# Matrix inversions on four partition groups, and the last one moved beside the output projection

## The chip, the cores and the metric

The kernel runs on one core of a Trainium2 chip. The core has five engines that work side by side, each with its own queue of instructions that it takes in order: TensorE (PE, matrix products), VectorE (DVE), ScalarE (ACT), GpSimd (POOL) and SyncE (SP, which here only issues transfers). Transfers between device memory (DRAM) and the core's memory (SBUF) are issued by ACT, POOL or SP into their own queues and carried by 16 DMA engines. The metric is the time of one execution on the device, in microseconds (us), as the median of several runs.

## The reference

The computation is a trunk of two layers over a sequence of 512 positions, with a model width of 1024. Cut to what matters:

```python
for l in range(DEPTH):                       # two layers
    h = rms_norm(x, norm_mix[l])
    if l % 2 == 0:                           # layer 0
        u = h @ w_in_even[e]
        ya = hgrn2_mix(aq, af, ai, ag, ...)  # columns of u
        yb = rwkv7_mix(ub, ...)              # the other columns
        y = jnp.concatenate([ya, yb], axis=-1) @ w_out_even[e]
    else:                                    # layer 1: S5 and mLSTM
        y = jnp.concatenate([yc, yd], axis=-1) @ w_out_odd[o_]
    x = x + y
    x = x + swiglu(rms_norm(x, norm_ffn[l]), ...)
return rms_norm(x, norm_final)
```

RWKV-7 is a recurrence over positions, in eight heads of 64:

```python
def step(state, inp):
    r_t, w_t, k_t, v_t, a_t, b_t = inp
    sa = jnp.einsum("bhvk,bhk->bhv", state, a_t)
    state = (state * w_t[:, :, None, :] + sa[..., None] * b_t[:, :, None, :]
             + v_t[..., None] * k_t[:, :, None, :])
    return state, jnp.einsum("bhvk,bhk->bhv", state, r_t)
```

## The kernel before

Weights stream from DRAM on SP's queue in pieces of 128 x up to 1024 (`raw`). Every matrix is split into a high and a low half (`hi` is a cast on ACT, L375; `lo` a subtraction, on DVE or POOL, L376), and each matrix product of two such operands is three products of 128 x 128 by 128 x 512 (`mm3`), all at line 292. `d`, `m` and `r` are the PSUM tiles: `d` of the large projections, `m` of HGRN2, `r` of RWKV-7; there are two `d` buffers.

Layer 0 runs three kinds of work side by side. The first is the input projection with HGRN2 (`dense`, F): lora parts L, RWKV-7's projections P0 to P3, HGRN2's blocks H0 to H3. HGRN2 forms decays `e` (POOL makes e from c, DVE multiplies them by u and k) which PE reads (m<-e), and a block's result `y` is stored to DRAM (scr_ya, L837). The second is RWKV-7 in chunks of 64 positions, for two halves g of the sequence and two groups q of four heads: `rwp` prepares (gates, keys, the triangular 64 x 64 blocks `pb`), `inv` is `rw_inverse`, and `rwd` is `rw_solve` for two pairs of heads, then `rw_chain` for both pairs beside each other. The third is the output projection.

`rw_prep` stores the diagonal 32 x 32 triangular blocks of `pb` to DRAM (scr_a, issued by ACT). `rw_inverse(q, g)` loads 32 of them on POOL's queue as `iu`, one block per partition, with 1024 elements each, and inverts each unit triangular block: at step j of 30, row j's multipliers times row j go to all rows above j. That is a product `ti` (L987) and an addition (L989) of j x (31 - j) elements on 32 partitions. It stores the inverse to scr_u (L991). `rw_solve` loads it as `ub` (L1000, eight transfers of 32 x 4 x 32, on POOL's queue), and PE multiplies (r<-y,ub), corrects by `amb` and multiplies again to give `wu`. `rw_chain` runs four chunks: PE sums a chunk (r<-kr,vbd, r<-pb,wu, r<-ar,hs), ACT and DVE copy half of it each to `sb`, PE transposes it (r<-con,sb, L1049), DVE scales it into the state `hs`. Then it normalises over a head (r<-kr,con, y, kr), multiplies by the gate (r<-la,lora) and leaves the result in `bon` (L1077).

Programs of these kinds of work are generators that yield a virtual cost. `weave` advances the stream with the least cost so far; `beside` alternates between streams, `then` runs one after the other, `scaled` multiplies the costs. The table `PRM` sets it all: `prog` lists the stages of layer 0, each woven to its end, with the place up to which F runs in it; `m` are the factors of inv, rwp and rwd; `e` is the factor of the RWKV-7 work beside the output projection; `dq` says which queue issues the transfers of the RWKV-7 part (ACT for scr_a's stores, POOL for the rest). The scheduler of the language then orders the instructions of each engine at build time.

In the kernel before, the last stage of `prog` is inv(1, 1) beside rwd(1, 0), with no F beside it. After the stages the eight x tiles are loaded (`xtiles`, L520, on ACT's queue, into the memory that HGRN2 has left). `outa` then reloads six of the eight 128-column groups of y from DRAM (`yraw`, L1164, on SP's queue, through two buffers), splits them into `ysp` (yhl[k]; the groups come in the order 0, 1, 2, 4, 5, 3, and 3 is H3's result), and runs, for each of the eight output tiles n, fifteen products of groups 0, 1, 2, 4, 5 (d<-ysp) and the addition to x[n] (L1173), which frees the `d` buffer. It is woven with the last rwd(1, 1). At the end the results of rwd(1, *) for groups 6 and 7 are split from `bon` into yhl[6] and yhl[7], and a second pass over n (weights wO0b) does the nine products of groups 3, 6 and 7.

The functions that the diff touches:

Of the kernel before, what the change touches and what calls it, by code (L numbers as in the profile page):

```python
# [198 lines left out]
PRM = {'c': (0, 1, 2, 3), 'seq': ['L', 'P0', 'P1', 'H0', 'P2', 'P3', 'H1', 'H2', 'H3'], 'm': {'inv': 1.728, 'rwp': 1.6, 'rwd': 0.675}, 'prog': [[('F', 'P1')], [('rwp', 0, 0), ('F', 'H0')], [('inv', 0, 0), ('rwp', 0, 1), ('F', 'P2')], [('inv', 0, 1), ('rwd', 0, 0), ('F', 'H1')], [('rwd', 0, 1), ('rwp', 1, 0), ('F', 'H2')], [('inv', 1, 0), ('rwp', 1, 1), ('F', 'H3')], [('inv', 1, 1), ('rwd', 1, 0)]], 'e': 0.2, 'k': 8.0, 'dq': 'aggg', 'j': 0.9, 'eng': {('h8', 2): 'G', ('c5', 0, 0): 'S', 'h7': 'G', 'c7': 'S', ('p2', 3, 0): 'S', ('c1', 0, 0): 'S', ('c1', 1, 0): 'S', 'c6': 'V', 'c4': 'S', ('c1', 2, 0): 'V', 'h3': 'V', ('p14', 3, 0): 'V', ('h8', 1): 'G', ('c7', 1): 'V', ('c5', 1): 'V', 'h5': 'V', ('c8', 2): 'G', ('p2', 0): 'S', ('s4', 1, 0): 'S', 's2': 'S', 'c2': 'S', 'z1': 'G', 'z4': 'G', 'z6': 'G', ('z5', 0): 'V', ('a6', 3): 'G', 'p10': 'V', 'z9': 'V', 'p13': 'S', ('z2', 1): 'G', ('z0', 4): 'S', ('z1', 3): 'V', 'h13': 'V', ('a6', 2): 'G', ('z0', 1): 'G', ('h12', 1): 'V', ('n2', 2): 'V', ('p11', 1): 'S', ('a2', 2): 'V'}, 'pu': (2, 4, 5, 6, 7, 9, 12, 13, 36), 'i': 1.0, 'h': 0.7, 'f': 1.4, 'pr': {}}  # L199
# [3 lines left out]
def trunk(ctx: ExitStack, tc: tile.TileContext, A, out, dbg=None, start=0):  # L203
# [451 lines left out]
    def layer0():  # L655
# [323 lines left out]
        def rw_inverse(q, g):  # L979

            iu = pl.tile([32, 32, 32], F32, tag="iu", name="iu")
            dq(1).dma_start(iu, scr_a[q, g].rearrange("p h b c s t -> (p h b c) s t"))
            G.memset(iu.rearrange("p a b -> p (a b)")[:, 0:1024:33], 1.0)
            for j in range(1, 31):
                n = 31 - j
                t3 = pl.tile([32, N2], F32, tag="ti", name="ti")[:, 0:j * n].rearrange("p (a b) -> p a b", b=n)
# [2 lines left out]
                G.tensor_tensor(iu[:, 0:j, j + 1:], iu[:, 0:j, j + 1:], t3, ADD)  # L989
# [759 lines left out]
```

## Time and profile before

| | |
|---|---|
| runs | 1464.06 us median of 3 (1461.65 to 1466.17) |
| profiled execution | 1462.31 us, of which the span of the trace is 1460.5 us |
| granted TensorE clock, mean | 0.976 of full speed |
| busy share of the span | PE 96%, PE weight loads 78%, DVE 66%, ACT 47%, POOL 24% |
| DMA | 133.39 MB, 91 GB/s on average |
| inversions on POOL, first to last operation, us from the start | 90.93 to 133.39, 156.37 to 193.60, 272.78 to 314.10, 333.60 to 375.02 |
| layer 0's last RWKV-7 product (r<-la,lora) | 409.86 us |

A row of the timeline gives the start, the duration, the engine, the line and what it writes from what it reads. "[0.62 <-DVE wu L281]" says that the engine had been idle for 0.62 us ahead of the row and that DVE's instruction at line 281 that writes wu released it. A group's row gives the busy time and the mean of one in ns, then the idle time ahead. TensorE's granted clock (PEclk) is the share of full speed that the chip allowed it in a stretch. Instructions that issue a transfer are not counted as busy.

### The profile page before, as it was taken

The numbers are of one execution on the slowest core, as the hardware profiler recorded it, in microseconds if no ns is written. First come the engines' busy times: TensorE is split into PE (matmuls) and PEld (weight loads), VectorE is DVE, ScalarE is ACT, GpSimd is POOL, SyncE is SP. The second block draws the span as 40 slices with busy tenths as digits, with TensorE's granted clock in tenths as the row PEclk, the third lists the DMA queues.
The fourth block names the chain that finished last, engine by engine and source line by source line (L and its number), as shares of the span: only waits on it lengthen the run. The fifth ranks groups of instructions, "written<-read, shape, count | busy, mean of one in ns | idle before, by whom it ended". The sixth has DMA issues, their size and how long they took to land.

```text
span 1460.5 us, 19910 instructions
## 1 busy us (share of the span) xinstructions
PE 1400.2 (96%) x6668; PEld 1136.9 (78%) x6668; DVE 961.2 (66%) x2041; ACT 681.1 (47%) x1594; POOL 354.0 (24%) x538
## 2 busy tenths in 40 slices
PE   8989999988999999999999899999999999999996
PEld 5877878766787788888888678766678888888885
DVE  7588679899688656555444688678776555554433
ACT  7554565636365333344333333477554434433332
POOL 5367650668420333110010542100020000000001
PEclk9988999999999999999999999999999999999998
DMA  5311221111323332333343842410133233333331
GB/s 180 94 38 46 64 72 52 30 46 58 118 84 97 101 116 91 113 108 106 105 125 105 206 113 80 116 58 28 56 105 90 99 101 96 92 102 94 93 114 61
DMA packets 51142, 133.39 MB, mean 91 GB/s; under 512 B 10640, under 2 KB 16272, under 8 KB 50784
## 3 DMA queue, kind: packets, MB, share of 16 engines
q1 hardware_dynamic: 38656, 116.86, 26.4%
q0 software_dynamic: 3024, 7.26, 2.1%
q10 hardware_dynamic: 9360, 8.00, 1.8%
q8 instruction: 53, 0.87, 0.2%
q14 instruction: 49, 0.40, 0.1%
HBM read 121.71 MB, written 10.39 MB: 90 GB/s over the span
## 4 chain that ended last, share of the span: by engine, by line
PE 76%; DVE 11%; POOL 4%; ACT 4%; DMA 2%; issue 2%; ACTq 0%; SPq 0%; DVEq 0%; POOLq 0%
PE d L292 63%; PE m L292 7%; PE r L292 5%; DVE lo L376 2%; POOL iu L989 1%; POOL ti L987 1%; DVE e L277 1%; DMA raw<-in_wV_dram 1%; ACT s L253 1%; DVE hl L467 1%; DVE ks L277 1%; ACT hi L375 0%; DVE u L277 0%; POOL ks L277 0%; DMA x<-in_xT_dram 0%
## 5 line engine op out<-in xcount | busy, mean ns | idle before, releaser
L375 ACT CAST hi<-raw 128x256 fp32r<-128x256 f32 (+1 forms) x809 | 317.4, 402 | 502.1 <-PE d L292 446.8
L376 DVE TENSOR_TENSOR lo<-raw,hi 128x256 fp32r<-128x256 f32 (+1 forms) x774 | 348.3, 460 | 280.5 <-ACT hi L375 269.6
L292 PE MATMUL d<-hh,hi 128*128 128x512 f32 x1088 | 436.1, 401 | 3.6 <-DVE ur L1086 2.4
L292 PE MATMUL d<-hh,lo 128*128 128x512 f32 x1088 | 431.4, 397 | 0.0
L292 PE MATMUL d<-hl,hi 128*128 128x512 f32 x1088 | 430.2, 395 | 0.0
L292 PEld LDWEIGHTS d<-hh,hi 128*128 128x128 f32 x1088 | 207.1, 190 | 48.0 <-DVE ur L1086 3.0
L292 PEld LDWEIGHTS d<-hh,lo 128*128 128x128 f32 x1088 | 206.8, 190 | 43.7 <-issue 1.5
L292 PEld LDWEIGHTS d<-hl,hi 128*128 128x128 f32 x1088 | 206.9, 190 | 43.3 <-issue 2.3
L292 PE MATMUL d<-ah,hi 128*128 128x512 f32 x330 | 128.4, 389 | 0.0
L292 PE MATMUL d<-al,hi 128*128 128x512 f32 x330 | 128.4, 389 | 0.0
L292 PE MATMUL d<-ah,lo 128*128 128x512 f32 x330 | 128.4, 389 | 0.0
L1718 POOL TENSOR_TENSOR x<-x,f 128x256 f32<-128x256 f32 x6 | 5.2, 889 | 358.8 <-issue 352.3
L292 PE MATMUL d<-ysp,hi 128*128 128x512 f32 x224 | 75.3, 411 | 2.7 <-DVE x L1685 1.5
L473 POOL TENSOR_TENSOR rstd<-rstd,sq 128x512 f32<-128x512 f32 x21 | 28.8, 1373 | 196.8 <-ACT sq L253 196.7
L989 POOL TENSOR_TENSOR iu<-iu,ti 32x30 f32<-32x30 f32 (+14 forms) x120 | 70.8, 590 | 9.2
L292 PEld LDWEIGHTS d<-ah,hi 128*128 128x128 f32 x330 | 61.9, 188 | 13.0
L292 PEld LDWEIGHTS d<-ah,lo 128*128 128x128 f32 x330 | 61.9, 188 | 12.8
L292 PEld LDWEIGHTS d<-al,hi 128*128 128x128 f32 x330 | 61.9, 188 | 12.8
L987 POOL TENSOR_TENSOR ti<-iu 32x30 f32<-32x30 f32 (+14 forms) x120 | 68.9, 574 | 9.0
L292 PEld LDWEIGHTS d<-ysp,hi 128*128 128x128 f32 x224 | 42.2, 193 | 12.9 <-DVE x L1685 2.3
L292 PE MATMUL d<-ysp,lo 128*128 128x512 f32 x112 | 45.5, 406 | 0.0
L1197 DVE TENSOR_TENSOR g<-d,g 128x512 f32<-128x512 f32 x42 | 29.0, 691 | 24.1 <-PE d L292 24.1
(490 smaller groups left out, 2043.0 us busy)
## 6 DMA issues: line engine op xcount, KB each, us to landing
raw<-in_wGU_dram SPq DMA_DIRECT2D x88, 512.0 KB, 3.6
raw<-in_wD_dram SPq DMA_DIRECT2D x32, 512.0 KB, 3.5
raw<-in_wA_dram SPq DMA_DIRECT2D x16, 512.0 KB, 3.7
raw<-in_wB_dram SPq DMA_DIRECT2D x13, 512.0 KB, 3.7
raw<-in_wD_dram SPq DMA_DIRECT2D x16, 384.0 KB, 3.1
raw<-in_wV_dram SPq DMA_DIRECT2D x6, 512.0 KB, 5.7
raw<-in_wQ_dram SPq DMA_DIRECT2D x6, 512.0 KB, 3.6
raw<-in_wK_dram SPq DMA_DIRECT2D x6, 512.0 KB, 3.7
```

The costliest lines, as they stand in the source:

```text
L253: a = S.activation(o, i, f, bias=bias, scale=scale)
L277: on(op, i, j).tensor_tensor(o, a, b, f)
L292: T.matmul(o, w, a, start=start, stop=stop)
L375: S.copy(h, src)
L376: eng.tensor_tensor(l, src, h.bitcast(F32), SUB)
L467: V.scalar_tensor_tensor(self.hl[:, k, :], x, pc(self.g, k), self.hh[:, k, :].bitcast(F32), MUL, SUB)
L473: self.eng.tensor_tensor(self.rstd, self.rstd, sq, ADD)
L987: G.tensor_tensor(t3, iu[:, j:j + 1, j + 1:].to_broadcast([32, j, n]), iu[:, 0:j, j:j + 1].to_broadcast([32, j, n]), MUL)
L989: G.tensor_tensor(iu[:, 0:j, j + 1:], iu[:, 0:j, j + 1:], t3, ADD)
L1197: V.tensor_tensor(g1, pu_, g1, MUL)
L1718: G.tensor_tensor(x[k][:, t], x[k][:, t], r_, MUL)
```

## The change

There are two edits. First, `rw_inverse` copies its 32 blocks four times, into four groups of 32 partitions (`iu`, 128 x 1024), and gives group k of the 32 rows those with r = k mod 4 to work on (`iw`, 128 x 8 x 32). A step's two operations then run on 128 partitions with m = (j+3)//4 rows each. The loads are eight instead of one, in pairs of one `iw` (eight rows of 32 elements per block, so pieces of 128 bytes) and one `iu`; at the end the four groups get their ones on the diagonal and are stored with four transfers. The step's cost in the weave is 0.6 instead of 1.2. Second, the last stage is taken out of `prog`, and its work stands at the head of the stream beside the output projection, whose factor e goes from 0.2 to 0.4.

```diff
 PRM = 
 ...
-[('inv', 1, 0), ('rwp', 1, 1), ('F', 'H3')], [('inv', 1, 1), ('rwd', 1, 0)]], 'e': 0.2,
+[('inv', 1, 0), ('rwp', 1, 1), ('F', 'H3')]], 'e': 0.4,
 ...
         def rw_inverse(q, g):
-            iu = pl.tile([32, 32, 32], F32, tag="iu", name="iu")
-            dq(1).dma_start(iu, scr_a[q, g].rearrange("p h b c s t -> (p h b c) s t"))
-            G.memset(iu.rearrange("p a b -> p (a b)")[:, 0:1024:33], 1.0)
+            iu = pl.tile([P, 32, 32], F32, tag="iu", name="iu")
+            iw = pl.tile([P, 8, 32], F32, tag="iw", name="iw")
+            blocks = scr_a[q, g].rearrange("p h b c s t -> (p h b c) s t")
+            for k in range(4):
+                w = slice(32 * k, 32 * k + 32)
+                dq(1).dma_start(iw[w], blocks.rearrange("n (r k) t -> n k r t", k=4)[:, k])
+                dq(1).dma_start(iu[w], blocks)
             for j in range(1, 31):
-                n = 31 - j
-                t3 = pl.tile([32, N2], F32, tag="ti", name="ti")[:, 0:j * n].rearrange("p (a b) -> p a b", b=n)
-                G.tensor_tensor(t3, iu[:, j:j + 1, j + 1:].to_broadcast([32, j, n]),
-                                iu[:, 0:j, j:j + 1].to_broadcast([32, j, n]), MUL)
-                G.tensor_tensor(iu[:, 0:j, j + 1:], iu[:, 0:j, j + 1:], t3, ADD)
-                yield 1.2
-            dq(2).dma_start(scr_u[q, g].rearrange("p h b c s t -> (p h b c) s t"), iu)
+                n, m = 31 - j, (j + 3) // 4
+                t3 = pl.tile([P, 80], F32, tag="ti", name="ti")[:, 0:m * n].rearrange("p (a b) -> p a b", b=n)
+                G.tensor_tensor(t3, iu[:, j:j + 1, j + 1:].to_broadcast([P, m, n]),
+                                iw[:, 0:m, j:j + 1].to_broadcast([P, m, n]), MUL)
+                G.tensor_tensor(iw[:, 0:m, j + 1:], iw[:, 0:m, j + 1:], t3, ADD)
+                yield 0.6
+            for k in range(4):
+                w = slice(32 * k, 32 * k + 32)
+                G.memset(iw[w].rearrange("p a b -> p (a b)")[:, k:256:36], 1.0)
+                dq(2).dma_start(scr_u[q, g].rearrange("p h b c s t -> (p h b c) s t")
+                                .rearrange("n (r k) t -> n k r t", k=4)[:, k], iw[w])
 ...
-        weave((scaled(rwd(1, 1), PRM.get("e", 1.0)), None), (outa(), "end"))
+        weave((scaled(build(("then", ("beside", ("inv", 1, 1), ("rwd", 1, 0)), ("rwd", 1, 1))), PRM.get("e", 1.0)), None), (outa(), "end"))
```

Lines below the inversion stand ten lines later in the changed kernel (L1049 becomes L1059, L1164 becomes L1174). PE, DVE, ACT and SP have the same instructions in both kernels; POOL has 52 more. On PE the order differs in two places only: beside the first inversion with H0, and from the last solution but one to the end of the RWKV-7 work.

The first place is POOL's queue at the last inversion, inv(1, 1) beside H3. In the kernel before, one load (`iu`) is followed by three of HGRN2's five operations on `e`, then by the inversion:

```order
L982 DMA iu<-scr_a 32x1024
L277 TENSOR_TENSOR e<-c 128x8x32
L277 TENSOR_TENSOR e<-c 128x16x16
L277 TENSOR_TENSOR e<-c 128x32x8
L983 MEMSET iu 32x32
L987 TENSOR_TENSOR ti<-iu 32x30
L989 TENSOR_TENSOR iu<-iu,ti 32x30
```

In the changed kernel, on POOL at the same place, eight loads stand among all five operations on `e`, ahead of the inversion:

```order
L987 DMA iw<-scr_a 32x8x32
L988 DMA iu<-scr_a 32x1024
L277 TENSOR_TENSOR e<-c 128x8x32
L277 TENSOR_TENSOR e<-c 128x16x16
L987 DMA iw<-scr_a 32x8x32
L277 TENSOR_TENSOR e<-c 128x32x8
L988 DMA iu<-scr_a 32x1024
L987 DMA iw<-scr_a 32x8x32
L277 TENSOR_TENSOR e<-c 128x64x4
L277 TENSOR_TENSOR e<-c 128x128x2
L988 DMA iu<-scr_a 32x1024
L987 DMA iw<-scr_a 32x8x32
```

Before, the other two operations on `e` stood after fourteen of the inversion's operations; now the first operation of the inversion stands behind all five and one more load of iu.

The second place is ACT's queue at the head of rwd(1, 0)'s chain, where `wu` is the end of the solution, `x` the loads of the x tiles and `sb` the copies that the chain waits for. The kernel before:

```order
L281 COPY wu_245<-r 64x8x64
L375 CAST hi<-raw 128x256
L375 CAST hi<-raw 128x128
L281 COPY sb_249<-r 64x64 x2
L281 COPY sb_247<-r 64x64
L375 CAST hi<-raw 128x256
L520 DMA x_3981<-in_xT_dram 128x512
L520 DMA x_3982<-in_xT_dram 128x512
L281 COPY sb_247<-r 64x64
L281 COPY sb_249<-r 64x64 x2
L520 DMA x_3983<-in_xT_dram 128x512
```

The changed kernel, on ACT from the same copy to wu (five of the eight loads are shown, they stand in a row):

```order
L520 DMA x_3768<-in_xT_dram 128x512
L520 DMA x_3769<-in_xT_dram 128x512
L520 DMA x_3770<-in_xT_dram 128x512
L520 DMA x_3771<-in_xT_dram 128x512
L520 DMA x_3772<-in_xT_dram 128x512
L375 CAST ysp<-yraw 128x512
L281 COPY sb_247<-r 64x64
L281 COPY sb_249<-r 64x64 x2
```

The eight loads, which stood between copies to sb, and the cast of the last reloaded group of y, which stood behind all of them, now stand ahead of the first copy to sb.

The third place is PE's queue where that chain makes its first transpose (r<-con,sb). In the kernel before, a few products of the output projection stand among the chain's:

```order
L292 MATMUL r_3809<-pb2_272,wu1_245 128x128
L292 MATMUL d_4162<-ysp_4025,hi_4049 128x512
L292 MATMUL d_4162<-ysp_4026,hi_4049 128x512
L292 MATMUL r_3809<-kr2_273,vbd2_275 128x128
L1049 MATMUL r_3814<-con_72,sb0_247 128x128
L292 MATMUL r_3801<-kr0_255,vbd0_257 128x128
```

In the changed kernel seventeen of them stand in a row there; the last of these rows on PE, with `d_4063` the third output tile and `d_4183` the fourth:

```order
L292 MATMUL d_4063<-ysp_3821,hi_3949 128x512
L292 MATMUL d_4063<-ysp_3822,hi_3949 128x512
L292 MATMUL d_4063<-ysp_3821,lo_3950 128x512
L292 MATMUL d_4183<-ysp_3797,hi_4051 128x512
L292 MATMUL d_4183<-ysp_3798,hi_4051 128x512
L1059 MATMUL r_3995<-con_72,sb0_247 128x128
L292 MATMUL r_3979<-kr0_255,vbd0_257 128x128
```

Counted over the whole region, 47 products of the output projection stood ahead of rwd(1, 1)'s first product with ub (r<-y1,ub0) and now 60 do. Behind the last r<-la,lora, 39 stood ahead of the first that reads yhl[6], and now 26 do.

More of the change, by code (lines that the diff above doesn't have):

```diff
@@ L196, in _layout @@
     return o
-PRM = {'c': (0, 1, 2, 3), 'seq': ['L', 'P0', 'P1', 'H0', 'P2', 'P3', 'H1', 'H2', 'H3'], 'm': {'inv': 1.728, 'rwp': 1.6, 'rwd': 0.675}, 'prog': [[('F', 'P1')], [('rwp', 0, 0), ('F', 'H0')], [('inv', 0, 0), ('rwp', 0, 1), ('F', 'P2')], [('inv', 0, 1), ('rwd', 0, 0), ('F', 'H1')], [('rwd', 0, 1), ('rwp', 1, 0), ('F', 'H2')], [('inv', 1, 0), ('rwp', 1, 1), ('F', 'H3')], [('inv', 1, 1), ('rwd', 1, 0)]], 'e': 0.2, 'k': 8.0, 'dq': 'aggg', 'j': 0.9, 'eng': {('h8', 2): 'G', ('c5', 0, 0): 'S', 'h7': 'G', 'c7': 'S', ('p2', 3, 0): 'S', ('c1', 0, 0): 'S', ('c1', 1, 0): 'S', 'c6': 'V', 'c4': 'S', ('c1', 2, 0): 'V', 'h3': 'V', ('p14', 3, 0): 'V', ('h8', 1): 'G', ('c7', 1): 'V', ('c5', 1): 'V', 'h5': 'V', ('c8', 2): 'G', ('p2', 0): 'S', ('s4', 1, 0): 'S', 's2': 'S', 'c2': 'S', 'z1': 'G', 'z4': 'G', 'z6': 'G', ('z5', 0): 'V', ('a6', 3): 'G', 'p10': 'V', 'z9': 'V', 'p13': 'S', ('z2', 1): 'G', ('z0', 4): 'S', ('z1', 3): 'V', 'h13': 'V', ('a6', 2): 'G', ('z0', 1): 'G', ('h12', 1): 'V', ('n2', 2): 'V', ('p11', 1): 'S', ('a2', 2): 'V'}, 'pu': (2, 4, 5, 6, 7, 9, 12, 13, 36), 'i': 1.0, 'h': 0.7, 'f': 1.4, 'pr': {}}
+PRM = {'c': (0, 1, 2, 3), 'seq': ['L', 'P0', 'P1', 'H0', 'P2', 'P3', 'H1', 'H2', 'H3'], 'm': {'inv': 1.728, 'rwp': 1.6, 'rwd': 0.675}, 'prog': [[('F', 'P1')], [('rwp', 0, 0), ('F', 'H0')], [('inv', 0, 0), ('rwp', 0, 1), ('F', 'P2')], [('inv', 0, 1), ('rwd', 0, 0), ('F', 'H1')], [('rwd', 0, 1), ('rwp', 1, 0), ('F', 'H2')], [('inv', 1, 0), ('rwp', 1, 1), ('F', 'H3')]], 'e': 0.4, 'k': 8.0, 'dq': 'aggg', 'j': 0.9, 'eng': {('h8', 2): 'G', ('c5', 0, 0): 'S', 'h7': 'G', 'c7': 'S', ('p2', 3, 0): 'S', ('c1', 0, 0): 'S', ('c1', 1, 0): 'S', 'c6': 'V', 'c4': 'S', ('c1', 2, 0): 'V', 'h3': 'V', ('p14', 3, 0): 'V', ('h8', 1): 'G', ('c7', 1): 'V', ('c5', 1): 'V', 'h5': 'V', ('c8', 2): 'G', ('p2', 0): 'S', ('s4', 1, 0): 'S', 's2': 'S', 'c2': 'S', 'z1': 'G', 'z4': 'G', 'z6': 'G', ('z5', 0): 'V', ('a6', 3): 'G', 'p10': 'V', 'z9': 'V', 'p13': 'S', ('z2', 1): 'G', ('z0', 4): 'S', ('z1', 3): 'V', 'h13': 'V', ('a6', 2): 'G', ('z0', 1): 'G', ('h12', 1): 'V', ('n2', 2): 'V', ('p11', 1): 'S', ('a2', 2): 'V'}, 'pu': (2, 4, 5, 6, 7, 9, 12, 13, 36), 'i': 1.0, 'h': 0.7, 'f': 1.4, 'pr': {}}
 @with_exitstack
```

## The prediction

> **What bounds the kernel now.** I read first the page's busy rows, then a table of stretches through layer 0, then what TensorE waited for there, and last the rows of the engines that the change touches.
>
> ```profile
> span 1460.5 us, 19910 instructions
> PE 1400.2 (96%) x6668; PEld 1136.9 (78%) x6668; DVE 961.2 (66%) x2041; ACT 681.1 (47%) x1594; POOL 354.0 (24%) x538
> ```
>
> TensorE (PE) is busy 96% of the span and the change removes no matmul, so it can win only PE's idle time and the time that PE runs at a lower clock, near the inversions. The next table shows how much there is; its columns are the length of the stretch, busy time of PE, weight loads, DVE, ACT and POOL, then PE's granted clock.
>
> ```profile
> core 0: us, PE busy (x) PEld busy (x) DVE busy (x) ACT busy (x) POOL busy (x), PEclk, DMA share, GB/s
> 88.00:142.00 54.00, 49.05 (x248) 40.06 (x247) 46.11 (x88) 31.45 (x79) 44.49 (x77) 0.84 0.14 40
> 142.00:214.00 72.00, 70.48 (x407) 58.19 (x405) 52.41 (x117) 40.16 (x104) 45.07 (x81) 1.00 0.25 72
> 258.00:342.00 84.00, 72.98 (x422) 59.91 (x419) 76.82 (x168) 47.93 (x121) 59.12 (x102) 0.88 0.14 39
> 342.00:384.00 42.00, 36.62 (x237) 30.14 (x237) 34.64 (x70) 18.85 (x50) 33.83 (x55) 1.00 0.34 111
> 384.00:410.00 26.00, 25.62 (x166) 21.64 (x166) 14.28 (x34) 10.43 (x32) 3.28 (x6) 1.00 0.18 54
> ```
>
> I call the first of these A, the second B, the third D, and the last two together E. Idle PE time is 4.95 us in A, 1.52 in B, 11.02 in D, 5.38 up to 384 us and 0.38 after it. Besides, the clock of 0.84 and 0.88 costs at most 0.16 x 49.05 = 7.8 us in A and 0.12 x 72.98 = 8.8 us in D. VectorE (DVE) is the fullest engine after PE: 76.82 of 84 us in D. And the waits of PE from 88 to 416 us name it:
>
> ```profile
> engine line waited for: us in total, times, longest us
> PE m L292 <- DVE e L277: 5.4, 7, 2.4
> PE r L959 <- ACT y L281: 5.1, 1, 5.1
> PE r L292 <- DMA ub<-scr_u: 1.2, 1, 1.2
> ```
>
> So PE waits for DVE's products far more than for an inversion. The one wait for a result of an inversion is 1.2 us; the other inversions have slack. A shorter inversion by itself is worth little, therefore; what counts is whether it gets out of DVE's way, and what the new order of the last region does.
>
> **The inversion on POOL.** Rows of POOL over 88 to 380 us, by shape, and the stretch of the last inversion:
>
> ```profile
> L277 POOL TENSOR_TENSOR e<-c 128x256 f32<-128x256 f32 x30 | 21.0, 720 | 54.0 <-PE r L1049 44.7 <-PE m L731 4.5 <-DVE u L277 3.4
> L1000 POOL DMA_DIRECT2D ub<-scr_u x24 | 13.1, 553 | 6.2 <-DMA scr_u<-iu 4.0 <-PE d L292 2.3
> L989 POOL TENSOR_TENSOR iu<-iu,ti 32x240 f32<-32x240 f32 x8 | 6.3, 792 | 0.6
> L989 POOL TENSOR_TENSOR iu<-iu,ti 32x30 f32<-32x30 f32 x8 | 2.1, 268 | 0.6
> L982 POOL DMA_DIRECT2D iu<-scr_a x4 | 2.2, 560 | 23.6 <-DMA scr_a<-pb 15.6 <-DVE e L281 7.7 <-PE d L292 0.4
> 333.60:375.02 41.42, 36.88 (x63) 0.98 0.26 84
> ```
>
> An operation on 128 partitions x 256 takes 720 ns, less than the 792 of 32 x 240: partitions cost nothing, elements do. Between 30 and 240 elements the time grows by 524 ns, 2.5 ns an element on a base of 193 ns. Step j works j(31-j) elements now, 4960 in all; with a quarter of the rows, rounded up, it works 1424. Two operations a step: before 60 x 0.193 + 9920 x 0.0025 = 36.4 us (the stretch shows 36.88 with three other operations in it), after 60 x 0.193 + 2848 x 0.0025 = 18.7 us. The gaps between the operations, 41.42 - 36.88 = 4.5 us, stay. Against the 17.7 us saved stand seven more loads at 0.56 us and three more stores at 0.55, with three memsets about 6 us. POOL is free about 12 us sooner per inversion; that hides behind the inversions' slack. What doesn't hide is DVE:
>
> ```profile
> L376 DVE TENSOR_TENSOR lo<-raw,hi 128x256 fp32r<-128x256 f32 x16 | 6.1, 420 | 0.0
> L277 DVE TENSOR_TENSOR e<-e,u 128x256 f32<-128x256 f32 x3 | 1.6, 543 | 0.0
> L277 DVE TENSOR_TENSOR e<-e,k 128x256 f32<-128x256 f32 x3 | 1.2, 414 | 0.0
> ...
> L277 DVE TENSOR_TENSOR e<-e,u 128x256 f32<-128x256 f32 x6 | 4.6, 786 | 0.0
> L277 DVE TENSOR_TENSOR e<-e,k 128x256 f32<-128x256 f32 x6 | 4.2, 707 | 0.0
> L376 DVE TENSOR_TENSOR lo<-raw,hi 128x256 fp32r<-128x256 f32 x7 | 3.7, 527 | 0.4 <-ACT hi L375 0.3
> ...
> L376 DVE TENSOR_TENSOR lo<-raw,hi 128x256 fp32r<-128x256 f32 x8 | 5.6, 727 | 0.7 <-ACT hi L375 0.7
> ...
> L376 DVE TENSOR_TENSOR ysp<-yraw,ysp 128x512 fp32r<-128x512 f32 x5 | 4.9, 1004 | 1.1 <-ACT ysp L375 1.1
> L376 DVE TENSOR_TENSOR lo<-raw,hi 128x256 fp32r<-128x256 f32 x5 | 4.4, 917 | 0.0
> ```
>
> These are DVE's groups in four stretches: 214 to 258 us, where POOL does nothing, then the first, third and last inversion (in A, D and E). The same split takes 420 ns alone and 527, 727 and 917 beside an inversion. Over the 420, 543 and 414 ns of the quiet stretch, A loses 7 x 0.107 + 6 x 0.243 + 6 x 0.293 = 4.0 us, D 8 x 0.307 = 2.5 us, and E 5 x 0.497 = 2.5 us and 5 x 0.31 for the ysp splits (0.69 us where POOL was idle, row below), 4.1 together. The Trainium skill, "SBUF — State Buffer", section "Who interferes with whom", has the two engines share a port pair that one holds for a whole instruction while the other fully blocks; the stretched rows agree with it in kind. By that rule each of the 60 operations could still catch a DVE operation, and shorter holds would save no more than the busy time that goes, which is what I use.
>
> I take the stretch to shrink with POOL's busy time, by 17.7/36.4 = half. **A**: 2.0 us of DVE time, on the engine that PE waits for, and of the 7.8 us of clock a share as the idle time goes, 2.0/4.95 = 40% or 3.1 at most; I take a third of that, since no row here tells how the clock follows an idle time: **-3 us**. Bounds: the whole 4.0 us and the whole 3.1, -7; or nothing gained and the three more loads (3 x 0.56) that now stand ahead of the first e operations on POOL paid in full, +2. **B**: 1.52 us of idle time is there: **-0.5** (-1 to +0.5). **D**: half of 2.5 is 1.3, and of the idle 11.02 us the 5.1 behind ACT's y stay, so clock gains 0.7: **-2** (-5 to +0.5).
>
> **The last region, E.** Here the order itself changes. Rows of PE, then DVE, then ACT, in order of time:
>
> ```profile
> 364.34 0.63 PE L292 MATMUL d<-ysp,hi 128*128 128x512 f32 x2
> 364.80 0.39 PE L292 MATMUL d<-ysp,lo 128*128 128x512 f32 x1
> ...
> 369.25 0.33 PE L1049 MATMUL r<-con,sb 128*128 128x128 f32 x1 [0.39 <-ACT sb L281]
> ...
> 373.70 0.73 PE L292 MATMUL d<-ysp,hi 128*128 128x512 f32 x2 [0.59 <-DVE x L1173]
> ...
> 381.96 0.65 PE L292 MATMUL r<-la,lora 96*128 96x256 f32 x2
> 383.83 1.13 PE L292 MATMUL r<-y,ub 128*128 128x128 f32 x8 [1.22 <-DMA ub<-scr_u]
> ...
> 410.18 0.82 PE L292 MATMUL d<-ysp,hi 128*128 128x512 f32 x2
> ```
> ```profile
> 362.54 0.60 DVE L281 COPY amb<-am 32x128 f32<-32x128 f32 x1
> ...
> 372.95 0.69 DVE L1173 TENSOR_TENSOR x<-x,d 128x512 f32<-128x512 f32 x1 [0.68 <-DMA x<-in_xT_dram]
> 378.89 0.69 DVE L376 TENSOR_TENSOR ysp<-yraw,ysp 128x512 fp32r<-128x512 f32 x1
> ...
> 417.30 0.42 DVE L376 TENSOR_TENSOR ysp<-bon,ysp 128x256 fp32r<-128x256 f32 x1
> ...
> 417.97 0.42 DVE L376 TENSOR_TENSOR ysp<-bon,ysp 128x256 fp32r<-128x256 f32 x1
> ```
> ```profile
> 369.13 0.42 ACTq L520 DMA_DIRECT2D x<-in_xT_dram  x1
> ```
>
> A product of the output projection (d<-ysp) takes 0.23 us of PE: two from 364.34 to 364.80. The region runs as a chain: the first chain of rwd(1,0) (its first transpose r<-con,sb at 369.25), its end (lora, 381.96), the last solution (r<-y,ub, 383.83), its chain, and the splits of yhl[6] and yhl[7], done at 417.72 and 418.39. The order puts 60 projection products ahead of the last r<-y,ub where there were 47, and 26 instead of 39 between the last lora (next product at 410.18) and the first one that reads yhl[6]. So 13 x 0.23 = 3.0 us of work is moved into the idle 5.38 us; but now the cover at the end is short. Before, 39 products ran from 410.18 to 419.1, past 418.39. After, 26 end at 416.1 and PE waits for 417.72: 1.6 us, a wait that takes the place of the one removed. If the last r<-y,ub starts when it did, E gains 3.0 - 1.6 = 1.4 us; it breaks even if r<-y,ub starts at 385.2.
>
> When does it start? In PE's new order 15 products of the third output tile and 2 of the fourth stand ahead of the first r<-con,sb. The third tile needs the PSUM buffer that x0's addition frees, and that needs x0's load. Before, the load went out at 369.13, after the last HGRN2 block's result was stored, and the addition ended at 373.64; 15 products take to 377.1, two more 377.5. ACT's order gives the same: all eight x loads and the cast of the last yraw stand ahead of the first sb copy. With nothing else earlier the first r<-con,sb is 8 us late. But the last block's tail has fewer DVE operations interleaved now (two copies to amb and one to wu stand elsewhere in DVE's order, about 2 us at the 0.60 of a row), and half of E's 4.1 us of stretch goes, so I take 4 us off: 373.5. From there the chain took 381.96 - 369.25 = 12.7 us with 21 products among it; it keeps 13, 1.8 us fewer, of which I take 1.2 since half of that chain waits on copies. Then r<-y,ub follows 0.65 us after the lora starts, its 1.22 us wait being gone: 373.5 + 11.5 + 0.65 = 385.65, so E is **+0.5 us**. Bounds: with none of the 4 us, +4.5; if the loads are early enough that the first r<-con,sb stays at 369.25, 381.4, or -3.8.
>
> **The sum.** -3 - 0.5 - 2 + 0.5 = -5 us. The profiled execution took 1462.31 us, 1.8 more than its span and 1.75 less than the median of the runs, 1464.06, so it would be 1457.3, and the median **1459 us**. All else of the program keeps its order and is taken at nothing: its cover is PE itself, full at 96%.
>
> **The rivals.**
> *All hidden.* Only 1.2 us waits for an inversion, and DVE's operations may collide with 60 short operations as with 60 long ones, since both have the same count; the 13 products moved forward are paid for at yhl[6]. Against it: the e<-e,k rows differ between stretches, so exposure matters. Time: within 2 us of 1464, taken 1462 to 1466. Chance 0.22.
> *More than I take.* If DVE's saturation in A and D is broken, PE's idle time there and the clock go together: up to -7 and -5, with E at -3.8, up to -17. For it: clock and idle time stand in the same stretches (0.84, 0.88 against 1.00 elsewhere). Against it: 5.1 us in D hangs on ACT. Time 1447 to 1456. Chance 0.20.
> *Slower.* The 15 + 2 products, the x loads and the cast put ahead of the sb copies hold the first r<-con,sb back; from r<-y,ub at 385.2 on each microsecond is lost, as PE is full behind it (25.62 of 26). With the loads as late as before this is +4.5; and POOL's issues in A ahead of the e operations +2 in place of -3, with D at +0.5. Sum +7, about 1471. It decides when the x0 load goes out later than 368 us and A gains nothing. A sentence of the same page and section speaks for it: DMAs issued by GpSimd have their descriptors starved while DVE holds the port, so eight small loads in DVE's fullest stretch would be late; the 0.56 us and the slack seen here show no such stall. Chance 0.15.
> *That it does not do what it says* is small: the order shows the operations in place, and only the gain in time is in doubt.
>
> **The numbers.** The forecast (-2 to -8) has 0.43. A measurement of this kernel tells about 0.3% from no change, 4.4 us: below 1459.7 is faster, above 1468.5 slower. Of my own case 0.27 lies below that and 0.16 within; the larger gain adds 0.20 to faster, the hidden case 0.22 to same, the slower rival 0.15 to slower: 0.47, 0.38, 0.15. Range: 1449 to 1470, leaving out the far ends of the larger gain and of the slower rival.
>
> **What would show it.** Right: an inversion of about 24 us on POOL between its first and last operation; DVE's lo splits beside it nearer 420 ns than 727 or 917; clock above 0.84 in A and 0.88 in D; r<-y,ub near 385.6 less what A to D gained; PE waiting some 1.6 us for DVE ysp L376 at the end. Wrong: DVE's splits unchanged beside the shorter inversion (then the all-hidden case), a PE wait of over 4 us ahead of the first r<-con,sb (then the slower one), or clock of 1.00 in A and D (then the larger gain).

## The result, and the profile after

The changed kernel takes 1452.74 us (median of 6 runs, 1448.62 to 1456.41), the kernel before 1464.21 us beside it: ratio 0.9921, with a 95% interval of 0.9900 to 0.9942. It is faster by 11.5 us; I had forecast 5. The profiled execution took 1456.41 us with a span of 1454.6 us, and is the slowest of the six.

The same table of stretches as before, for the changed kernel (A, B, D and the two parts of E; length, busy time of PE, weight loads, DVE, ACT and POOL, then the granted clock):

```profile
88.00:142.00 54.00, 51.24 (x259) 41.92 (x258) 41.34 (x95) 31.66 (x80) 36.30 (x89) 0.84 0.19 52
142.00:214.00 72.00, 69.66 (x395) 57.58 (x394) 47.62 (x113) 41.91 (x109) 37.28 (x94) 0.97 0.30 78
258.00:342.00 84.00, 76.19 (x477) 63.49 (x479) 75.24 (x185) 53.63 (x132) 58.18 (x128) 0.94 0.22 57
342.00:384.00 42.00, 37.60 (x240) 31.55 (x241) 27.12 (x67) 18.64 (x51) 24.10 (x60) 1.00 0.39 119
384.00:410.00 26.00, 26.00 (x159) 21.92 (x158) 15.75 (x37) 12.42 (x38) 0.74 (x1) 1.00 0.15 47
```

PE is idle 2.76 us in A instead of 4.95 and 7.81 in D instead of 11.02; the clock in D is 0.94 instead of 0.88, in A it is still 0.84. These windows are the same times and not the same work (the third holds 477 products instead of 422), so the gain is read below from stretches that are cut at events. DVE's busy time over the whole program falls by 25 us, from 961.2 (by 20 us in a second execution of the changed kernel, e6 below):

```profile
PE 1402.0 (96%) x6668; PEld 1139.8 (78%) x6668; DVE 936.1 (64%) x2041; ACT 681.6 (47%) x1594; POOL 324.6 (22%) x590
```

The waits of PE from 88 to 416 us have lost the one for an inversion's result (ub) and two for DVE, which stand in the same view of the kernel before as the three rows that the prediction shows:

```profile
PE m L292 <- DVE st L810: 2.8, 2, 2.2
PE d L292 <- DVE ur L1086: 2.3, 1, 2.3
```

In the changed kernel these are gone, and a wait of 2.8 us for the addition to x is new:

```profile
PE r L959 <- ACT y L281: 4.6, 1, 4.6
PE m L292 <- DVE e L277: 4.3, 6, 2.0
PE d L292 <- DVE x L1183: 3.1, 2, 2.8
```

DVE's groups beside the first inversion (A), beside the third (D) and beside the last (E) answer to the stretched rows of before:

```profile
L376 DVE TENSOR_TENSOR lo<-raw,hi 128x256 fp32r<-128x256 f32 x8 | 3.5, 451 | 2.0 <-ACT hi L375 2.0
L277 DVE TENSOR_TENSOR e<-e,k 128x256 f32<-128x256 f32 x6 | 3.2, 532 | 0.0
L277 DVE TENSOR_TENSOR e<-e,u 128x256 f32<-128x256 f32 x6 | 2.6, 435 | 1.7 <-ACT e L253 1.7
...
L376 DVE TENSOR_TENSOR lo<-raw,hi 128x256 fp32r<-128x256 f32 x10 | 4.4, 474 | 0.0
...
L376 DVE TENSOR_TENSOR ysp<-yraw,ysp 128x512 fp32r<-128x512 f32 x5 | 3.5, 722 | 0.6 <-ACT ysp L375 0.6
L376 DVE TENSOR_TENSOR lo<-raw,hi 128x256 fp32r<-128x256 f32 x6 | 2.6, 455 | 0.0
```

The lo splits, which took 527, 727 and 917 ns, take 451, 474 and 455; the e operations fall from 786 and 707 to 435 and 532. So not half of the stretch of these rows has gone but about three quarters in A and D (in D 10 x 0.054 = 0.5 us is left of 2.5), and more in E.

To see where the time came from I cut layer 0 at four events that both orders share: the first load of an inversion in A, in B and in D on POOL, PE's r<-con,raw after its wait for ACT's y (the second one of the last preparation), and PE's last r<-la,lora. For the changed kernel three of these rows are:

```profile
147.32 0.59 POOL L987 DMA_DIRECT2D iw<-scr_a  x1 [10.93 <-DMA scr_a<-pb]
...
270.39 0.59 POOL L987 DMA_DIRECT2D iw<-scr_a  x1 [5.09 <-DMA scr_a<-pb]
```
```profile
324.67 1.06 PE L959 MATMUL r<-con,raw 128*64 128x128 f32 x4 [4.55 <-ACT y L281]
...
404.63 0.60 PE L292 MATMUL r<-la,lora 96*128 96x256 f32 x2
```

and for the kernel before:

```profile
268.10 0.51 POOL L982 DMA_DIRECT2D iu<-scr_a  x1 [5.07 <-DMA scr_a<-pb]
```
```profile
332.22 1.06 PE L959 MATMUL r<-con,raw 128*64 128x128 f32 x4 [5.15 <-ACT y L281]
...
409.86 0.67 PE L292 MATMUL r<-la,lora 96*128 96x256 f32 x2
```

The last lora is not the same point of the work in both orders, as 13 products of the output projection (3.0 us of PE) have moved from behind it to ahead of it. So I add an event ahead of which both orders have done the same work: the first product of the second pass over n, the 121st of the projection (8 tiles of 15 come first). Its rows, before and then changed:

```profile
418.56 0.61 PE L292 MATMUL d<-ysp,hi 128*128 128x512 f32 x2
```
```profile
410.31 0.62 PE L292 MATMUL d<-ysp,hi 128*128 128x512 f32 x2
```

With the first loads of the inversions in A and B (88.19 and 151.10 before, 87.13 and 147.32 after), this gives the lengths of the stretches in us. E is given up to the last lora and up to the second pass. The table holds the experiments too, whose labels are explained below:

| profiled execution | A | B and C | D | E, to the last lora | E, to the second pass | from the last lora to the end |
|---|---|---|---|---|---|---|
| before | 62.9 | 117.0 | 64.1 | 77.6 | 86.3 | 1050.6 |
| changed | 60.2 | 123.1 | 54.3 | 80.0 | 85.6 | 1050.0 |
| changed, again (e6) | 60.2 | 116.8 | 54.4 | 79.9 | 85.5 | 1047.8 |
| inversion alone (e1) | 60.1 | 116.7 | 57.1 | 76.9 | 85.6 | 1046.1 |
| inversion alone (e7) | 60.2 | 117.0 | 57.6 | 77.5 | 86.2 | 1046.7 |
| move alone (e2) | 64.7 | 117.1 | 61.9 | 90.0 | 91.3 | 1047.1 |
| products twice in B, D (e3) | 60.2 | 118.9 | 55.1 | 85.7 | 91.3 | 1047.3 |
| long holds in B, D (e5) | 61.6 | 116.9 | 58.6 | 84.9 | 90.5 | 1042.6 |

A gains 2.7 us, D gains 9.8, and E gains 0.7 up to the second pass; the 2.4 us that it is longer up to the last lora are less than the 3.0 us of work that has moved there. B and C gain nothing; the 6.1 us that they lose in the profiled execution are a stretch from 208 to 224 us in which the clock stood at 0.50 to 0.66, and which the second profile of the same kernel does not have. The last column varies by 8 us, where the moved products are 3.0 us of work (7.6 in e2), and the time ahead of A, which is not in the table, varies by 5 us (87 to 92). That shows how far a single profile can be trusted.

### The profile page after: what moved, and what is told of

Read it like the earlier page. It is cut to its first block, busy times and chain, and to the rows that moved or that the text cites. A ratio compares the mean times of both kernels' runs of the same rounds, so it can differ in the third digit from the quotient of the medians.

```text
span 1454.6 us, 19968 instructions
## 1 busy us (share of the span) xinstructions
PE 1402.0 (96%) x6668; PEld 1139.8 (78%) x6668; DVE 936.1 (64%) x2041; ACT 681.6 (47%) x1594; POOL 324.6 (22%) x590
## 4 chain that ended last, share of the span: by engine, by line
PE 81%; DVE 10%; ACT 4%; issue 2%; POOL 1%; DMA 1%; ACTq 0%; DVEq 0%; SPq 0%; POOLq 0%
PE d L292 66%; PE m L292 9%; PE r L292 5%; DVE lo L376 1%; DVE e L277 1%; ACT s L253 1%; DVE hl L467 1%; DVE ks L277 1%; ACT hi L375 1%; DMA x<-in_xT_dram 1%; DMA raw<-in_wA_dram 0%; DVE u L277 0%; POOL ks L277 0%; ACTq L952 0%; DVE hst L277 0%
## 5 line engine op out<-in xcount | busy, mean ns | idle before, releaser
L376 DVE TENSOR_TENSOR lo<-raw,hi 128x256 fp32r<-128x256 f32 (+1 forms) x774 | 340.2, 450 | 281.9 <-ACT hi L375 278.0
L292 PEld LDWEIGHTS d<-ah,lo 128*128 128x128 f32 x330 | 61.9, 188 | 13.0
L292 PEld LDWEIGHTS d<-ah,hi 128*128 128x128 f32 x330 | 61.9, 188 | 12.8
L292 PEld LDWEIGHTS d<-al,hi 128*128 128x128 f32 x330 | 61.9, 188 | 12.8
L992 POOL TENSOR_TENSOR ti<-iu,iw 128x60 f32<-128x60 f32 (+10 forms) x120 | 42.8, 357 | 20.6 <-DMA iu<-scr_a 9.1
L994 POOL TENSOR_TENSOR iw<-iw,ti 128x60 f32<-128x60 f32 (+10 forms) x120 | 43.6, 363 | 9.4
```

Source lines behind the costliest of these rows:

```text
L292: T.matmul(o, w, a, start=start, stop=stop)
L376: eng.tensor_tensor(l, src, h.bitcast(F32), SUB)
L992: G.tensor_tensor(t3, iu[:, j:j + 1, j + 1:].to_broadcast([P, m, n]), iw[:, 0:m, j:j + 1].to_broadcast([P, m, n]), MUL)
L994: G.tensor_tensor(iw[:, 0:m, j + 1:], iw[:, 0:m, j + 1:], t3, ADD)
```

## The experiments

### Inversion and move apart

The first run has the new `rw_inverse` with the table and the weave of before, the second the inversion of before with the new table and weave:

```diff
 e1: the new rw_inverse;  prog ends with [('inv', 1, 1), ('rwd', 1, 0)], 'e': 0.2
 e2: the old rw_inverse;  prog ends with [..., ('F', 'H3')],             'e': 0.4
```

> Only the new inversion: the last stage stays in prog, e stays 0.2, so the order of the last region is that of the kernel before (26 projection products ahead of the first r<-con,sb, 47 ahead of the last r<-y,ub). Theory (the gain is the shorter inversion, by DVE's stretch and the clock in A and D; the move to the projection costs about 1 us): about 1452, within 2 us of the changed kernel, or 1 to 2 us below it. Rival (the gain is the move): 1461 to 1464.

> Only the move, with the inversion of before on 32 partitions and one load. Theory: the inversion now ends as late as before and 76 projection products stand ahead of the last r<-y,ub, so 1464 to 1469, no gain. Rival (the gain is the move): about 1453 to 1457.

Measured: the inversion alone 1448.38 us, ratio to before 0.9901 (0.9883 to 0.9920); the move alone 1470.82 us, 1.0066 (1.0048 to 1.0085). The gain is the inversion's; the move by itself costs 9 us, more than the 5 at most that I expected of it. In the run with the move alone the old inversion stores its result as late as before (43.0 us after r<-con,raw, 43.1 before), while more products of the projection stand ahead of what needs it:

```profile
373.59 0.54 POOL L991 DMA_DIRECT2D scr_u<-iu  x1 [0.29 <-POOL iu L989]
```
```profile
369.59 2.07 PE L292 MATMUL r<-pb,wu 128*128 128x128 f32 x8 [2.70 <-DVE wu L281]
...
378.11 0.27 PE L1049 MATMUL r<-con,sb 128*128 128x128 f32 x1
...
426.84 1.65 PE L292 MATMUL d<-ysp,hi 128*128 128x512 f32 x3 [3.04 <-ACT ysp L375]
```

The chain's first transpose starts at 378.11 us, 47.5 us after r<-con,raw (330.63), where the kernel before needed 37.0 (369.25 - 332.22). Up to the second pass E takes 91.3 us, 5.0 more than before. Behind it the cover at the end is too short: PE waits 3.04 us for a split of the last results (ysp), where the kernel before waits for nothing. A fall of the clock to 0.50 for 6.8 us goes with each of the waits of 2.70 and 3.04 us, at 368 and 426 us. The move is the new place of the work and the step of e from 0.2 to 0.4 together; no run tells the two apart.

To set the changed kernel and the inversion alone side by side, both ran once more on one chip:

> The changed kernel itself, to stand on the same chip beside the inversion alone. Theory (the move costs 1 to 4 us): 2 us or more above the inversion alone. Rival (the move is free): within 1.5 us of it.

> Only the new inversion, again, beside the changed kernel. Theory: 2 us or more below the changed kernel, PE without a wait for x0's addition of over 1 us. Rival (the move is free): within 1.5 us of it.

Measured: 1451.06 us, 0.9915 (0.9891 to 0.9939), and 1450.00 us, 0.9907 (0.9881 to 0.9933). The intervals overlap almost wholly: the time agrees with the rival, and PE's wait for the addition to x is 2.2 us in the inversion alone too, where I had expected none. Up to the last lora E is shorter in the order of before (76.9 and 77.5 against 80.0 and 79.9), but that is the 3.0 us of moved work; up to the second pass the two orders are alike (85.6 and 86.2 against 85.6 and 85.5). The 1.1 us between the medians aren't resolved.

### What of POOL's work DVE feels

Two runs lengthen POOL's part of the second and third inversions, one with 30 short operations each (9 us of POOL's busy time), one with six long ones (8 us). The order on PE, DVE, ACT and SP is that of the changed kernel.

```diff
 e3, in the step (q != g)
-                G.tensor_tensor(t3, iu[...], iw[...], MUL)
+                for _ in range(2):
+                    G.tensor_tensor(t3, iu[...], iw[...], MUL)
 e5, after the step
+                if q != g and j % 5 == 0:
+                    G.tensor_tensor(iu[:, 0:20], iu[:, 0:20], rst64[:, 1:2] (one, broadcast), MUL)
```

> The changed kernel with each product of the second and third inversions (in B and D) made twice, so 30 more short POOL operations in each, about 10 us, which brings D's inversion back to the length of before; the order on PE, DVE, ACT and SP is the same row for row, and the results of these two inversions have 15 us or more of slack. Theory (POOL's time beside DVE is what costs): D's gain of about 9 us goes by half or more, 1457 to 1462. Rival (the gain comes from the order in which POOL's loads and e operations stand, or from the shorter inversion's earlier result): within 2 us of the changed kernel.

> The changed kernel with six extra operations of 128 x 640 elements (iu times one) in each of the second and third inversions, in place of the 30 short ones of the run with products made twice: about the same 10 us more on POOL, but 3840 elements instead of 1424 and 6 operations instead of 30; the order on the other engines is again the same. That run kept DVE's lo splits in D at 488 ns although POOL was as long busy as before. Theory (the stretch goes by the elements that POOL moves, not by its busy time or its number of operations): lo splits in D at 600 ns or more and 2 to 4 us slower than the run with short ones, about 1459 to 1461. Rival (the stretch goes by the number of operations that meet): lo splits at or below 480 ns and the same time.

Measured: 1457.03 us, 0.9972 (0.9956 to 0.9987), with the short ones; 1456.02 us, 0.9959 (0.9940 to 0.9978), with the long ones. By the ratios both lose 5 to 8 us against the changed kernel (0.9915 and 0.9921), as the theory had it for the first, but not for its reason. With the short operations D takes 55.1 us, within a microsecond of the changed kernel. The time goes in E (91.3 us to the second pass instead of 85.6), where the e operations of the last HGRN2 block stand behind the inversion in POOL's queue; POOL and PE in that run:

```profile
324.10 3.79 POOL L1011 DMA_DIRECT2D ub<-scr_u  x7 [0.18 <-issue]
...
329.04 1.23 POOL L277 TENSOR_TENSOR e<-c 128x256 f32<-128x256 f32 x2
```
```profile
332.27 1.94 PE L292 MATMUL m<-e 128*128 128x64 f32 x8 [6.80 <-DVE e L277]
```

In the changed kernel that wait is 0.47 us. So a longer inversion costs once the next block's operations queue behind it, and 30 more short operations beside DVE cost nothing that shows in D. The long operations do show: D takes 58.6 us, 4.2 more than in the changed kernel, and all of it is idle time of PE (10.5 us against 6.2), with this wait in it:

```profile
310.45 0.70 PE L292 MATMUL r<-c,con 128*128 128x256 f32 x2 [2.70 <-DVE c L932]
```

Two of my bounds were wrong. The lo splits take 470 ns, not 600 or more, and the medians don't show the 2 to 4 us that the long operations were to cost over the short ones (1456.02 against 1457.03 us). Other DVE operations took the hit: e<-e,k takes 776 ns against 522 with the short ones, and two operations of 0.40 us (the ones that write a) took 1.34 and 1.49 us; each began 0.24 us after a long operation of POOL and ended 0.15 and 0.27 us after its end. Rows of e<-e,k of 270 to 318 us, long and then short:

```profile
L277 DVE TENSOR_TENSOR e<-e,k 128x256 f32<-128x256 f32 x4 | 3.1, 776 | 0.0
```
```profile
L277 DVE TENSOR_TENSOR e<-e,k 128x256 f32<-128x256 f32 x4 | 2.1, 522 | 0.0
```

The same question was put to the first two inversions, where nothing of HGRN2 stands behind within 10 us:

```diff
 e9, inversions of q = 0
+                m = max(m, min(8, 164 // n))     # more rows of the same operations
 e10, inversions of q = 0
+                for _ in range(2):               # each product twice
```

> The changed kernel with more rows per step in the first two inversions (A and B): up to eight per group, as far as 164 elements go, where the extra rows add zero times row j; 3189 elements instead of 1424 in each of the two operations of an inversion, the same 60 operations and transfers, about 9 us more on POOL; the order elsewhere is the same, and no e operation and no result needed within 10 us stands behind. Theory (DVE's stretch goes by the elements that POOL moves): DVE's total busy time 4 us or more above the run beside it with short operations, the e groups in A above 500 and 600 ns again, 1453 to 1456. Rival (elements don't matter, only POOL's queue does): the same as the changed kernel, 1451.

> The changed kernel with each product of the first two inversions made twice: 30 more short operations each, about 10 us more on POOL with 1424 elements more, and nothing of HGRN2 behind them in the queue. Theory (short operations beside DVE are nearly free; the 6.8 us that PE waited for DVE e in the run with the second and third inversions so lengthened was POOL's queue, which here has slack): within 1.5 us of the changed kernel. Rival (POOL's busy time beside DVE costs): 3 us or more above it.

Measured: 1456.49 us, 0.9944 (0.9924 to 0.9964), and 1457.20 us, 0.9940 (0.9918 to 0.9961). In DVE's rows of A the theory holds in part. With more elements, which took 5 us more of POOL per inversion and not 9, e<-e,k takes 632 ns and lo 526 (the changed kernel: 532 and 451); with 9 us more in short operations they take 525 and 485. But the other e group, e<-e,u, stays at 458 ns, below both bounds that I gave, and DVE's total busy time is 945.6 us against 941.9, 3.7 more where I expected 4. The rows of e<-e,k, more elements and then short:

```profile
L277 DVE TENSOR_TENSOR e<-e,k 128x256 f32<-128x256 f32 x6 | 3.8, 632 | 0.0
```
```profile
L277 DVE TENSOR_TENSOR e<-e,k 128x256 f32<-128x256 f32 x6 | 3.1, 525 | 0.0
```

In the order of the length of one POOL operation the four kernels line up: e<-e,k in A takes 707 ns before (165 elements a POOL operation on average), 632 with more elements (106), and 532 and 525 in the changed kernel and with the products twice (47 in both, though the second has half as many elements again). So neither the number of operations nor the sum of elements sets the stretch in these rows; the length of a single operation fits.

In time the theory does not hold: A takes 60.4 and 61.4 us against 60.2, and by the ratios both kernels end some 3 us above the changed one, the one that should be free no less than the other. Both profiles have D at 57.0 and 57.1 us, with a fall of the clock at 285 us that the changed kernel's two profiles lack. That fall comes in some executions and not in others though the order in D is the same, as is shown further below, so it tells little of these two changes. Why both end 3 us above the changed kernel, and the free run with them, stays open.

### The chain behind the x loads

```diff
 e4, in outa
-            for k in (0, 1, 2, 4, 5, 3):
+            for k in (0, 1, 2, 4, 5):
 ...
             for n in range(KD):
+                if n == 5:
+                    group(3)                     # reload and split of group 3
```

> The changed kernel with the reload and the split of y's group 3 written ahead of the sixth output tile instead of ahead of the first: the cast no longer stands ahead of the first sb copies on ACT; the 15 projection products that need x0's addition still stand ahead of the first r<-con,sb on PE. Theory (x0's addition gates PE, the cast only comes at about the same time): within 1.5 us of the changed kernel. Rival (the cast on ACT is what holds the chain): 3 us or more below it.

Measured: 1453.69 us, 0.9945 (0.9929 to 0.9961), no better than the changed kernel (by the ratios 3 to 4 us above it, which is outside the 1.5 that I gave, with intervals that overlap), and E takes 80.3 us against 80.0 to the last lora, 85.9 against 85.6 to the second pass. The cast is not what holds the chain; PE still waits for the addition to x, as its row in that run says:

```profile
358.60 1.03 PE L292 MATMUL d<-ysp,hi 128*128 128x512 f32 x2 [2.45 <-DVE x L1188]
...
363.74 0.28 PE L1059 MATMUL r<-con,sb 128*128 128x128 f32 x1
```

### Fewer transfers, and other queues

```diff
 e8, e11: iu in one transfer that reads the blocks four times
+            dq(1).dma_start(iu, blocks.unsqueeze(0).to_broadcast([4, 32, 32, 32]))
 e8 alone: iw in one, and the store in one
+            dq(1).dma_start(iw, blocks.rearrange("n (r k) t -> k n r t", k=4))
 e12: scr_a's stores on SP
-'dq': 'aggg'
+'dq': 'sggg'
```

> Only the new inversion, with its eight loads made two (one for iw, one for iu that reads the blocks four times) and its four stores one: nine POOL issues fewer per inversion, about 5 us, and no loads between the e operations. Theory (POOL's queue counts where the next e operations stand behind it, in D and E): 1 to 3 us below the inversion alone. Rival (hidden by slack, or one large transfer lands later than eight small ones): the same within 1 us, or slower.

> Only the new inversion, with iu's four loads made one that reads the blocks four times (128 pieces of 4 KB), iw's four loads and the four stores kept. In the run with three transfers the merged iw load (1024 pieces of 128 bytes) and the merged store landed after up to 14.6 and 10.4 us. If only the transfers of many short pieces suffer: the same as the inversion alone or up to 2 us below it (three issues fewer per inversion). If any merged transfer suffers: iu lands 5 us or more later than now and the time is 3 us or more above the inversion alone.

> Only the new inversion, and the 32 stores of the blocks to scr_a issued by SP instead of ACT. In every run so far PE waits 4.6 to 5.1 us once for ACT's copy to y, while ACT issues eight such stores in 3.9 to 4.6 us ahead of it. Theory (those issues are what holds the copy): the wait falls below 1.5 us and the time stands 3 to 5 us below the inversion alone, 0.987 of before. Rival (the copy waits for PE's transposes, or SP's weight loads now stand behind the stores): the wait moves elsewhere and the time is within 2 us of the inversion alone.

Measured, all with the inversion alone as their base: three transfers 1471.54 us, 1.0058 (1.0038 to 1.0079), slower than the kernel before; one iu load 1452.76 us, 0.9916 (0.9892 to 0.9939); stores on SP 1446.78 us, 0.9884 (0.9851 to 0.9918). Merging was a mistake. The merged iw load takes 2.1 to 2.3 us to issue, it lands after 7.1 to 7.6 us, the merged iu load after 10.9 to 14.6 and the merged store after 8.2 to 10.4. (The 14.6 us that the expectation of the second of these runs gives for iw are iu's.) The inversion in A can't start until 102.89 us, where it starts at 99.17 in the inversion alone, and E takes 95.2 us to the second pass:

```profile
87.33 2.28 POOL L985 DMA_DIRECT2D iw<-scr_a  x1 [0.40 <-issue]
...
102.89 0.24 POOL L990 TENSOR_TENSOR ti<-iu,iw 128x30 f32<-128x30 f32 x1 [7.06 <-DMA iu<-scr_a]
```

With iu alone merged, that load lands after 8.8 to 12.5 us, where four took 2.4 to 5.6 each (the last line of what the trace says of each; one merged load, then four in e6):

```profile
DMA to landing us min/median/max: 8.8/9.4/12.5
```
```profile
DMA to landing us min/median/max: 2.4/2.8/5.6
```

So any merged transfer suffers, large pieces or small. The 3 us or more that this was to cost don't show: by the ratio the run with iu alone merged lies 0.1% above the inversion alone, within the intervals. With the stores on SP the wait for ACT's y was to fall below 1.5 us. It is gone ahead of r<-con,raw, but one of 4.2 us stands at another line, as the rival had it, so the theory behind that run is wrong as it stands. Its median is the lowest of all, but its interval overlaps that of the inversion alone (0.9881 to 0.9933), and the order on PE changed with it:

```profile
PE r L971 <- ACT y L281: 4.2, 1, 4.2
```

The inversion alone and the run with stores on SP are clearly below the kernel before; that either beats the changed kernel is not shown.

## Why the prediction was right and where it was wrong

**The bound and the direction** were right: the gain came from DVE and the clock beside the inversions, not from waits for their results, and the move to the projection brought nothing. The time lies in the range, at its lower part; the gain is more than twice the forecast. The stretches give 2.7 us in A, about 7 in D when like is set beside like (below), and 0.7 in E, about 10 of the 11.5.

**The inversion on POOL.** I had 18.7 us of busy time and 23 to 24 us from first to last operation. In B it is 18.77 us in 24.37 (with two memsets); in A, D and E it takes 26.3, 29.7 and 28.8 us, and in D it is 24.91 us busy, so POOL is stretched beside DVE too:

```profile
99.44:125.77 26.33, 21.59 (x62) 0.68 0.12 40
157.00:181.37 24.37, 18.77 (x62) 1.00 0.15 45
280.34:310.06 29.72, 24.91 (x61) 1.00 0.12 37
331.00:359.75 28.75, 21.60 (x62) 0.98 0.29 85
```

**DVE's stretch.** The step "I take the stretch to shrink with POOL's busy time, by half" failed, and so did the count of it. Of the rows that were counted about a quarter of the stretch is left, as POOL's operations are shorter (2848 elements of 9920, 29%, in as many operations). But three groups in A and one in D were not all that was stretched: DVE's busy time falls from 54.8 to 47.1 us in A, where the forecast was 2.0, and from 58.2 to 50.3 us in D, where it was 1.3. The Trainium skill, "SBUF — State Buffer", "Who interferes with whom", has the loser of the shared port pair blocked for the other's whole instruction. The long operations, of 1.25 to 1.71 us each, agree with that, down to the two operations that ended just behind them. That each of 60 operations could still catch one, which I took as a reason for the hidden case, does not: 30 more of them in each of two inversions left DVE's busy time at 937.4 us, against 936.1 and 941.4 in the changed kernel.

**A** was right in size (-2.7 against -3), and that was luck: the 1.0 us of clock did not come (0.84 both times), and the 7.7 us that DVE is less busy there shorten PE's idle time by 1.7 (from 5.0 to 3.3), mostly as the wait of 2.3 us for ur is gone, which the prediction did not price. The new inversion also changes the order on PE and DVE between 94 and 175 us, in every run that has it, so in A the shorter operations and the order are not told apart. **B** was -0.5 and is nothing.

**D** is the term that was mis-sized: -2 forecast, -9.8 measured. The order on PE and DVE is the same in D in both kernels. In the kernel before, the clock falls to about half twice in D:

```profile
284.00:288.00 4.00, 4.00 (x18) 0.56 0.00 0
288.00:292.00 4.00, 4.00 (x12) 0.59 0.01 2
...
296.00:300.00 4.00, 1.75 (x8) 0.76 0.27 82
300.00:304.00 4.00, 4.00 (x16) 0.50 0.00 0
304.00:308.00 4.00, 4.00 (x18) 0.88 0.00 0
```

The shares missing from 1.00 add up to 4 x (0.44 + 0.41) = 3.4 us for the first and 4 x (0.24 + 0.50 + 0.12) = 3.4 for the second, 6.8 together, and the changed kernel has neither. The rest is PE's idle time, 3.4 us less (9.6 before, 6.2 after; a part of the falls passed while PE was idle), and the long holds put 4.2 back. I had allowed the clock 0.7 us in D, as a share that goes with the idle time. It goes in steps instead. The second fall goes with a wait of 2.25 us, which is gone since DVE is on time and which the prediction did not price:

```profile
298.81 0.69 PE L292 MATMUL m<-u,st 128*128 128x64 f32 x2 [2.25 <-DVE st L810]
```

The first follows no wait at all, and the change does not decide it. In every trace the granted clock changes on a grid of 3.41 us, and the grid lies at another place against the program in each execution. Thirteen of the fourteen executions have the same order on PE in D (all but e12). I counted from one product of PE at the head of D (r<-ek,ak, at 278.09 us in the kernel before) to the next line of the grid. The six executions with the first fall (before, e1, e4, e7, e9, e10) have that line 2.9 to 3.4 or 0.1 to 0.3 us behind the product, the seven without it (changed, e2, e3, e5, e6, e8, e11) 0.5 to 1.9 us. The order in D is the same among both. So whether the first fall comes goes with where the grid happens to lie, and that both profiles of the changed kernel lack it is luck; why the clock falls there at all, with PE busy, stays open. Like beside like, the new inversion gains 6.5 to 7.1 us in D with the first fall (64.1 before; 57.0 to 57.6 in e1, e4, e7, e9 and e10), and 7.6 us without it (61.9 in the move alone, 54.3).

**E** was -3.8 to +4.5 with +0.5 taken, and is -0.7 up to the second pass. The path came out as described, and the sizes that were off cancel. PE's and ACT's rows of the changed kernel, from the addition to x to the last solution:

```profile
363.82 0.73 PE L292 MATMUL d<-ysp,hi 128*128 128x512 f32 x2 [2.85 <-DVE x L1183]
...
367.81 0.27 PE L1059 MATMUL r<-con,sb 128*128 128x128 f32 x1
...
379.23 1.12 PE L292 MATMUL r<-y,ub 128*128 128x128 f32 x8
```
```profile
359.05 4.25 ACTq L520 DMA_DIRECT2D x<-in_xT_dram  x8
```

Counted from r<-con,raw, x0's load goes out 2.5 us earlier than before (34.4 against 36.9), where I took 4; the first transpose comes 6.1 us later (43.1 against 37.0), where I took 4.25; from there to the last r<-y,ub it takes 11.4 us, where I took 12.15. The 1.6 us that PE was to wait for yhl[6] at the end are not there: that tail ends 6.05 us after the last lora (the split ends at 410.68), not 7.86 as I carried over from the trace of before, and its first reader starts at 410.99:

```profile
410.27 0.41 DVE L376 TENSOR_TENSOR ysp<-bon,ysp 128x256 fp32r<-128x256 f32 x1
```

**The rivals.** "All hidden" is out. "More than I take" is what happened, in D; that A's clock would go with it was wrong. The mechanism of "slower" was there, as the first r<-con,sb came 6.1 us later, but the 13 moved products paid for it; with the old inversion it decides, and the move alone is 9 us slower. Its eight small loads were not late: they land after 2.0 to 6.5 us, half of them within 2.8.

## What to carry to other kernels

A helper engine's work can hide fully from the critical path by the waits and still cost, as it slows a busy engine beside it. Look for the same operation at two mean durations in two stretches of the trace: the difference, times its count, is what the helper costs the busy engine, and all stretched groups belong in the sum. Shorter operations took three quarters of it away here although their number stayed. An order that was chosen for one length of a step is to be tried again when that length changes: the same move costs 9 us with the long inversion and nothing that could be measured with the short one. And two stretches are compared at a point ahead of which the same work is done, and in more than one execution, before a fall of the clock in one of them is put down to the change.

## What the runs showed of the hardware

- A tensor_tensor of POOL on 32 partitions took 268 ns for 30 elements of a partition and 792 for 240, about 0.2 us and 2.5 ns an element; on 128 partitions it was no dearer (237 ns for 30, 355 for 72, 726 for 256).
- Beside POOL's short operations (0.2 to 0.4 us for the most part) DVE's e<-e,k took 525 to 551 ns in A and lo 438 to 485, against 414 and 420 where POOL did nothing, and 30 more short ones did not raise them by more than 34 ns; beside operations of 1.25 to 1.71 us e<-e,k grew from 522 to 776 ns in D, and single operations of 0.40 us took up to 1.49.
- One POOL transfer of 512 KB in 128 pieces of 4 KB lands after 8.8 to 12.5 us, and four of 128 KB in 2.4 to 5.6 us each; one of 1024 pieces of 128 bytes takes 2.1 to 2.3 us to issue, and four of 256 pieces about 0.59 us each.
- The granted clock is 1.00 or 0.50 in these traces and changes on a grid of 3.41 us, whose place against the program differs between executions of one kernel. A fall lasts 3.4 to 20.5 us. Some falls go with a wait of PE of 2 to 3 us; one, at 284 us in the kernel before, follows no wait, and it comes or not with the place of the grid (thirteen executions).
